# Inverting a delta rule's 16-row blocks: a DRAM scratch and substitution on GpSimd, or selecting products and substitution on VectorE

## The chip, the cores and the metric

The kernel runs on one core of one Trainium2 chip. The metric is the device time of one execution, in microseconds. A core has five engines with an instruction queue each, in order: TensorE (PE, with its weight loads PEld), VectorE (DVE), ScalarE (ACT), GpSimd (POOL) and SyncE (SP), which issues most of the DMAs. An instruction that waits holds up everything behind it on its engine.

## What is computed

Two layers on a sequence of 256 tokens of width 1024. Each layer has a half-step gated feed-forward (FFN1), a mixing sub-layer, and another feed-forward (FFN2), each with its modulation (shift, scale and gate from a product of a small vector with `w_ada`). The mixing sub-layer projects its normalised input once and gives the columns to three groups of heads:

```python
u_conv, u_moba, u_gdn = jnp.split(u, [IN_CONV, IN_CONV + IN_MOBA], axis=-1)
y_conv = conformer_conv(u_conv, ...)         # gated, causal depthwise convolution of 31 taps, LayerNorm, silu
y_moba = moba_attention(partial_rope(mq, pos), partial_rope(mk, pos), mv)        # 6 heads of 64
qkv = jax.nn.silu(causal_depthwise_conv(qkv, gdn_conv_w))                        # 4 taps
o = gated_delta_net(l2norm(gq), l2norm(gk), gv, g, beta)                         # 6 heads of 64
```

The gated delta net works in four chunks of 64 tokens. With `decay` from the cumulated g of a chunk, it needs for each head and chunk the inverse T of a unit lower triangular 64x64 matrix:

```python
L = jnp.where(strict, jnp.einsum('bhncd,bhnsd->bhncs', k_beta, k) * decay, 0.0)
T = lax.linalg.triangular_solve(eye + L, jnp.broadcast_to(eye, L.shape), left_side=True, lower=True)
u = T @ v_beta
```

## The kernel before

Weights stream from DRAM in 1 MB pieces (`raw`) through SP's queue; four such buffers are in use. ACT rounds each piece to a high half (`hi`) and DVE subtracts it for the low half (`lo`), and PE takes three products of the halves (H is the input's). Products of the input projection that feed the delta rule are whole (`pm<-Y,raw`, fp32). In the feed-forward parts that is nearly all the work. In the mixing sub-layer, PE's projections are the carrier and the rest is woven in between.

The order of all instructions is fixed when the program is built, by a list scheduler. The class `Clock` (l. 80 to 174) keeps a modelled time of each engine and DMA queue; `cost` (l. 117) prices an instruction. In `mixing` (l. 1010) twelve generators stand beside the projections (`sides`, l. 1656): `key_norms`, `query_norms`, `decays`, `pairs`, `gate_conv`, `values_beta`, `inverse`, `delta_rule`, `attention`, two of `taps` and `convolution`. Between two matmul groups, `tick` (l. 1660) lets each of them go on whose awaited tiles are ready by the modelled clock. So prices and waits in the generators set where an instruction stands on its engine; at run time each engine goes through its list.

The parts that the change touches:

- `decays` (l. 1197) makes the decay factors of all heads: three products of the triangle `kc` with g (`spread`, tiles `Lb` and `S6a`, DVE), matmuls with `gt`, `ones` and `identb`, and 18 exponentials on ACT into `PT`. It begins when the keys' norm is done (`until("g", "kh")`).
- `pairs` (l. 1257) has PE multiply keys by keys for each head (`pa<-S3a`); DVE multiplies the result by the decay into `LD` and `LX` (the tile `xin_LT`). Then it writes the 32x32 diagonal blocks of L, 12 of them in each of 4 groups of 32 partitions, to a DRAM scratch `scr_l`, by 4 DMAs from POOL's queue.
- `inverse` (l. 1367) reads each 16x16 diagonal block back, by 2 DMAs, into one lane: `Lb` has 96 lanes of 256 numbers. POOL masks the off-diagonal 16-blocks (`Um`), then does forward substitution in all lanes at once, 15 steps of a product `T<-W,Lb` and a subtraction `W<-W,T`. The inverses and their transposes go to `scr_w` by 4 DMAs and come back block-diagonal as `Wc` by 2. From there PE joins 16-blocks to 32 (`pa<-Wc,Lb`) and 32 to 64 by small products.
- `taps` (l. 1523) does the long convolution, 31 taps for each of two tiles. A tap is one operation on DVE (`cacc<-hc,colB,cacc`), or a scaled copy on ACT (`ctap`, two buffers) and an addition on POOL (`cacc<-cacc,ctap`); the modelled clocks choose. While the substitution is on POOL, `cfg["lo_pool"]` holds the taps to DVE.
- `scr_w` is zeroed once, after the first feed-forward.

Other names: `v`, `Q` and `S3a` are the delta rule's value, query and key channels in their short convolution; `H` x8 on DVE are the low halves of the mixing input; `E` are the attention's exponentials, `F` and `V` tiles of its last product; `adaacc` and `px` are the next modulation's product, `mod` its result; `g_g` is g in the delta rule.

## Time and profile before

| | |
|---|---|
| time, three runs | 1201.04, 1201.66, 1204.4 us; median 1201.66 |
| profiled execution | 1202.57 us, its span 1200.8 us |
| mean granted TensorE clock | 0.976 |
| busy: PE, DVE, ACT, POOL | 1130.7, 874.4, 612.6, 169.3 us |
| mixing sub-layer, layer 1 and 2 | about 233 to 464, and 815 to 1030 us |
| POOL from the first write of scr_l to the last read, layer 1 and 2 | 298.9 to 334.3, and 880.8 to 916.6 us |

All instructions are recorded through one helper, so each row of the profile has line L171, and groups are told apart by their tiles: `out<-in`. A row of a timeline has its start, its length, the engine, the operation, the count of like instructions in a row (x2), and in brackets the engine's idle time ahead of it with what ended that time. A matmul of whole 32-bit numbers shows as two records of the profile. A window has its length, the busy time of each engine with its count of instructions, the clock that TensorE was granted (1.00 is full), the DMA share and the rate.

### The profile page before, as it was taken

The numbers are of one execution on the slowest core, as the hardware profiler recorded it, in microseconds if no ns is written. First come the engines' busy times: TensorE is split into PE (matmuls) and PEld (weight loads), VectorE is DVE, ScalarE is ACT, GpSimd is POOL, SyncE is SP. The second block draws the span as 40 slices with busy tenths as digits, with TensorE's granted clock in tenths as the row PEclk, the third lists the DMA queues.
The fourth block names the chain that finished last, engine by engine and source line by source line (L and its number), as shares of the span: only waits on it lengthen the run. The fifth ranks groups of instructions, "written<-read, shape, count | busy, mean of one in ns | idle before, by whom it ended". The sixth has DMA issues, their size and how long they took to land.

```text
span 1200.8 us, 22053 instructions
## 1 busy us (share of the span) xinstructions
PE 1130.7 (94%) x9085; PEld 1052.0 (88%) x9085; DVE 874.4 (73%) x1314; ACT 612.6 (51%) x1049; POOL 169.3 (14%) x213
## 2 busy tenths in 40 slices
...
GB/s 320 246 186 319 309 299 309 256 113 192 95 137 91 176 176 285 322 243 326 291 218 170 324 313 266 278 300 74 186 140 73 141 108 140 287 257 211 195 139 36
DMA packets 167661, 256.52 MB, mean 214 GB/s; under 512 B 8272, under 2 KB 134056, under 8 KB 167560
## 3 DMA queue, kind: packets, MB, share of 16 engines
...
q0 software_dynamic: 1024, 2.16, 0.9%
...
q14 instruction: 30, 0.25, 0.1%
...
## 4 chain that ended last, share of the span: by engine, by line
PE 71%; DVE 12%; ACT 6%; POOL 6%; issue 3%; DMA 1%; SPq 0%; POOLq 0%; DVEq 0%; ACTq 0%
PE pm L171 45%; PE pa L171 25%; DVE lo L171 3%; DVE adaacc L171 3%; PE px L171 2%; ACT hi L171 1%; POOL W L171 1%; POOL cacc L171 1%; POOL T L171 1%; POOL Lb L171 1%; DVE mod L171 1%; ACT L171 1%; DVE tmp L171 1%; DVE Lb L171 1%; DVE Y L171 1%
## 5 line engine op out<-in xcount | busy, mean ns | idle before, releaser
L171 PE MATMUL pm<-H,hi 128*128 128x256 f32 x2816 | 507.7, 283 | 2.8 <-issue 1.6
L171 DVE TENSOR_TENSOR lo<-raw,hi 128x1024 fp32r<-128x1024 f32 (+1 forms) x300 | 362.1, 1226 | 131.8 <-ACT hi L171 131.3
L171 PEld LDWEIGHTS pm<-H,hi 128*128 128x128 f32 x2816 | 431.9, 189 | 5.9 <-issue 2.2
L171 ACT CAST hi<-raw 128x1024 fp32r<-128x1024 f32 (+1 forms) x306 | 311.3, 1040 | 195.3 <-PE pm L171 80.7
L171 PE MATMUL pm<-H,lo 128*128 128x256 f32 x1408 | 392.4, 280 | 1.2 <-DVE lo L171 1.2
L171 PEld LDWEIGHTS pm<-H,lo 128*128 128x128 f32 x1408 | 264.5, 189 | 1.7 <-DVE lo L171 1.6
L171 PE MATMUL pa<-Y,hi 128*128 128x256 f32 x1312 | 241.3, 286 | 4.5 <-DVE xT L171 4.5
L171 PEld LDWEIGHTS pa<-Y,hi 128*128 128x128 f32 x1312 | 204.1, 192 | 6.7 <-DVE xT L171 5.3
L171 PE MATMUL pa<-Y,lo 128*128 128x256 f32 x656 | 185.8, 283 | 0.0
L171 PEld LDWEIGHTS pa<-Y,lo 128*128 128x128 f32 x656 | 127.3, 194 | 0.0
L171 POOL TENSOR_TENSOR xin_LT<-xin_LT 128x256 f32<-128x256 f32 x35 | 27.1, 775 | 664.8 <-ACT xin_LT L171 662.4
L171 ACT CAST Y<-tmp 128x256 fp32r<-128x256 f32 x88 | 35.8, 406 | 131.5 <-DVE tmp L171 131.5
L171 DVE SCALAR_TENSOR_TENSOR adaacc<-raw,c_act,adaacc 128x1024 f32<-128x1024 f32 x70 | 95.5, 1365 | 1.6
L171 DVE SCALAR_TENSOR_TENSOR Lb<-raw,c_act,Lb 128x1024 f32<-128x1024 f32 x56 | 71.8, 1283 | 4.2 <-DMA raw<-in_w_ada_dram 3.0
L171 POOL TENSOR_TENSOR cacc<-cacc,ctap 128x256 f32<-128x256 f32 x54 | 52.3, 973 | 122.0 <-DVE cacc L171 112.8
L171 DVE TENSOR_TENSOR Y<-tmp,Y 128x256 fp32r<-128x256 f32 x88 | 37.4, 425 | 41.5 <-ACT Y L171 41.5
L171 PE MATMUL pm<-Y,raw 128*128 128x256 f32 x288 | 66.8, 384 | 0.0
L171 PEld LDWEIGHTS pm<-Y,raw 128*128 128x128 f32 x288 | 53.4, 190 | 8.9 <-issue 1.0
L171 PE MATMUL pa<-hi,Y 128*128 128x512 f32 x176 | 54.8, 393 | 0.0
L171 ACT ACTIVATE tmp<-pm 128x256 f32<-128x256 f32 x84 | 31.8, 378 | 43.9 <-PE pm L171 43.7
L171 DVE TENSOR_REDUCE mod<-px 128x4 f32<-128x512 f32 x34 | 23.4, 689 | 34.3 <-PE px L171 34.2
L171 DVE SCALAR_TENSOR_TENSOR cacc<-hc,colB,cacc 128x256 f32<-128x256 f32 x66 | 36.0, 562 | 10.3 <-POOL cacc L171 9.4
...
## 6 DMA issues: line engine op xcount, KB each, us to landing
...
```

The lines of the kernel that those rows point to most:

```text
L171: return getattr(real, op)(*args, **kw)
```

## The change

No DRAM scratch is left, and none of its 24 DMAs of the two layers or the 2 that zero it. A block gets into its lane by products on PE that select. DVE multiplies L's blocks by a mask (`blk16`: which 16 rows a partition belongs to), which puts each block's rows apart in a column of its own, `S6a`; 16 matmuls against `sel` then gather row i of all 96 blocks. Back, the inverse is spread by the masks `col8` (three products on DVE, one on POOL) and gathered by 16 matmuls against `col12`; two scaled copies on DVE (`half`) and a transpose by 32x32 blocks give `Wc`. The masks add 48 columns to the constants.

The 16-block is split into two 8-blocks, whose substitution takes 7 steps for both at once, with DVE in place of POOL; two products of 512 numbers a lane, each with a sum over the innermost axis, give the off-diagonal 8-block. The masks `Um` are now scaled copies on ACT. `decays` begins with the keys' convolution (`kconv`) and waits for the norm's table (`ktable`) ahead of its exponentials and for `kh` ahead of its last table load. `lo_pool` isn't toggled any more, and some prices in `cost` are others: ACT, POOL, and DVE's small operations.

```diff
...
+    k[:, o["sel"]:o["sel"] + 16] = i[:, None] % 16 == np.arange(16)[None, :]
+    k[:, o["blk16"]:o["blk16"] + 8] = i[:, None] // 16 == np.arange(8)[None, :]
+    k[:, o["half"]:o["half"] + 2] = i[:, None] % 32 // 16 == np.arange(2)[None, :]
+    k[:, o["col12"]:o["col12"] + 12] = i[:, None] // 8 == np.arange(12)[None, :]
+    k[:, o["col8"]:o["col8"] + 8] = i[:, None] % 8 == np.arange(8)[None, :]
...
             rows = 4 * max(m, n) if kind == F32 else max(2 * m, n) if kind == F32R else max(64, n)
             return 0.0065 + rows * 0.000435
         if engine == "act":
-            return 0.1 + n * 0.00082 if n > 400 else 0.1 + n * 0.0011
+            return 0.1 + n * 0.00092 if n > 400 else 0.12 + n * 0.0013
         if engine == "gp":
-            return max(0.17, 0.08 + n * 0.00222)
+            return max(0.17, 0.08 + n * 0.0035)
         if op == "reciprocal":
             return 0.07 + n * 0.0063
-        return 0.11 + n * 0.00113 if op == "scalar_tensor_tensor" else 0.13 + n * 0.00105
+        return 0.11 + n * 0.00113 if op == "scalar_tensor_tensor" else 0.13 + n * 0.00105 if n > 64 else 0.22
 
...
@@ -1003,8 +1010,6 @@
         return closing(acc, [key + ("d", f) for f in last], [hp(f) for f in last], gate, following)
 
 
-    scr_l = nc.dram_tensor("scr_l", [12, 4, 32, 32], F32, kind="Internal").ap()
-    scr_w = nc.dram_tensor("scr_w", [2, 12, 4, 32, 32], F32, kind="Internal").ap()
     late = {}
 
     def mixing(l, G, normed, nxt):
@@ -1179,6 +1184,7 @@
 
             def back():
                 act.preload_act_table_set("natural_log_exp_and_others")
+                ev["ktable"] = True
                 yield from ()
 
             yield from norms((kh[:, 0:2], kh[:, 2:3]), lambda: act.preload_act_table_set("silu_and_others"), back, 1.0)
@@ -1195,7 +1201,7 @@
             ev["qh"] = True
 
         def decays():
-            yield from until("g", "kh")
+            yield from until("g", "kconv")
             g, lnbeta = ev["g"], ev["lnbeta"]
             while any(job[1].tensor.name.startswith("Lb") for job in ada_wait):
                 extract()
@@ -1227,6 +1233,7 @@
                     mm(x, onesr, R[:, :, k, 1], k == 0, k == 1)
                 if b == 0:
                     spread(2)
+                yield from until("ktable")
                 yield (x,)
                 let_go(d)
                 let_go(x)
@@ -1236,6 +1243,7 @@
                     act.activation(PT[:, h, 128:256], x[:, s], AF.Exp, bias=cross[:, h:h + 1])
                     act.activation(PT[:, h, 256:384], d[:, s, 1], AF.Exp, bias=lnbeta[:, 1, NH + h:NH + h + 1])
                     ev["decay", h] = True
+            yield from until("kh")
             act.preload_act_table_set("silu_and_others")
             ev["silu2"] = True
 
@@ -1260,10 +1268,6 @@
                 yield from until(("decay", h))
                 yield (kh, PT[:, h])
                 yield from products(h, kh)
-            yield (LD,)
-            for q in range(4):
-                c = slice(32 * q, 32 * q + 32)
-                qd.dma_start(out=scr_l.rearrange("g b j i -> b j g i")[q], in_=LD.rearrange("p h t x -> p (h t) x")[c, :, c])
             ev["LT"] = True
             yield from until("qh")
             for h in range(NH):
@@ -1354,8 +1358,8 @@
                 dve.tensor_tensor(w[:, 0], og[:, b], h[:, 0], op=OP.subtract)
             ev["gdn_done"] = True
 
-        W = sb([96, 2, 16, 16], "W")
-        sp.dma_start(out=W[:, 0].rearrange("p c i -> p (c i)"), in_=t["konst"][0:96, K_OFF["winit"]:K_OFF["winit"] + 256])
+        W = sb([96, 272], "W")
+        sp.dma_start(out=W[:, 0:256], in_=t["konst"][0:96, K_OFF["winit"]:K_OFF["winit"] + 256])
         QUAD = [slice(32 * q, 32 * q + 32) for q in range(4)]
 
         def put(dst, src, scale=1.0):
@@ -1369,36 +1373,72 @@
 
 
             yield from until("LT")
-            cfg["lo_pool"] = False
             buf = sb([128, 1024], "Lb")
-            Lb = buf[0:96, 0:256].rearrange("p (j i) -> p j i", i=16)
-            Um, X = (buf[:, o:o + 384].rearrange("p (m i) -> p m i", i=32) for o in (256, 640))
...
+            Um, X = (buf[:, o:o + 384].rearrange("p (m i) -> p m i", i=32) for o in (384, 0))
+            LM = LD.rearrange("p h t x -> p (h t) x")
+            gp.memset(Um[:, :, 0:16], 0.0)
             yield (LD,)
-            LM = LD.rearrange("p h t x -> p (h t) x")
+
+            def pair_up(x):
+
+                return x.rearrange("p (s y) -> p s y", s=2)[:, :, 0:128].rearrange("p s (c i) -> p s c i", i=16)[:, :, 0:8, 0:8]
+
+
+            E = sb([128, 16, 12, 8], "S6a")
+            blocks = LM.rearrange("p m (b i) -> p i m b", i=16)
+            for c in range(4):
+                n = slice(4 * c, 4 * c + 4)
+                dve.tensor_tensor(E[:, n], blocks[:, n], K["blk16"].unsqueeze(1).unsqueeze(1).to_broadcast([128, 4, 12, 8]), op=OP.mult)
             for q in QUAD:
...
+                act.activation(Um[q, :, 16:32], LM[q, :, q.start + 16:q.stop], AF.Copy, scale=K["half"][q, 0:1])
+            yield (E[:, 0:8],)
+            yield from room()
+            p = pside([96, 16, 16], True)
+            for i in range(16):
+                mm(p[:, i], E[:, i].rearrange("p m b -> p (m b)"), K["sel"], True)
+            yield soon(p, "dve")
+            let_go(p)
+            U = buf[0:96, 0:272]
+            dve.tensor_scalar(U[:, 0:256], p.rearrange("p i j -> p (i j)"), -1.0, None, op0=OP.mult)
+            V = W[:, 0:256].rearrange("p (c i) -> p c i", i=16)
+            V2, U2 = pair_up(W), pair_up(U)
+            for j in range(7):
+                n, ni = j + 1, 7 - j
+                T = sb([96, 2, n, ni], "T", bufs=2)
+                dve.tensor_tensor(T, V2[:, :, 0:n, j:j + 1].to_broadcast([96, 2, n, ni]),
+                                  U2[:, :, n:8, j:j + 1].rearrange("p s i o -> p s o i").to_broadcast([96, 2, n, ni]), op=OP.mult)
+                dve.tensor_tensor(V2[:, :, 0:n, n:8], V2[:, :, 0:n, n:8], T, op=OP.add)
+            U = U[:, 0:256].rearrange("p (i j) -> p i j", j=16)
+            cube, half8 = [96, 8, 8, 8], sb([96, 8, 8], "T", bufs=2)
+            for n in range(2):
+                x = tmp([128, 2, S]).rearrange("p a s -> p (a s)")[0:96].rearrange("p (c i a) -> p c i a", c=8, i=8)
+                if n == 0:
+                    dve.tensor_tensor(x, V[:, 0:8, 0:8].unsqueeze(2).to_broadcast(cube), U[:, 8:16, 0:8].unsqueeze(1).to_broadcast(cube), op=OP.mult)
+                else:
+                    dve.tensor_tensor(x, half8.unsqueeze(2).to_broadcast(cube),
+                                      V[:, 8:16, 8:16].rearrange("p b i -> p i b").unsqueeze(1).to_broadcast(cube), op=OP.mult)
+                dve.tensor_reduce(V[:, 0:8, 8:16] if n else half8, x, axis=AX.X, op=OP.add)
+
             C = sb([128, 2, 12, 32], "Wc")
...
+            F = sb([96, 12, 8, 16], "S6a"), tmp([128, 2, S]).rearrange("p a s -> p (a s)")[0:96].rearrange("p (i b c) -> p i b c", i=4, b=8)
+            VT = V.rearrange("p c i -> p i c")
+            Fs = []
+            for c in range(4):
+                x = F[0][:, 4 * c:4 * c + 4] if c < 3 else F[1]
+                Fs.append(x)
+                (gp if c == 3 else dve).tensor_tensor(
+                    x, VT[:, 4 * c:4 * c + 4].unsqueeze(2).to_broadcast([96, 4, 8, 16]),
+                    K["col8"][0:96].unsqueeze(1).unsqueeze(3).to_broadcast([96, 4, 8, 16]), op=OP.mult)
+            yield (Fs[1],)
+            yield from room()
+            p = pside([128, 16, 12], True)
+            for i in range(16):
+                mm(p[:, i], Fs[i // 4][:, i % 4].rearrange("p b c -> p (b c)"), K["col12"][0:96], True)
+            yield soon(p, "dve")
+            let_go(p)
+            for n in range(2):
+                dve.tensor_scalar(C[:, 0, :, 16 * n:16 * n + 16], p.rearrange("p i m -> p m i"), K["half"][:, n:n + 1], None, op0=OP.mult)
+            dve.transpose(C[:, 1].rearrange("p m i -> p (m i)"), C[:, 0].rearrange("p m i -> p (m i)"))
             yield from until("kh")
             wide = sb([128, 1536], "S6a")
             TA, X64 = (wide[:, o:o + 768].rearrange("p (m i) -> p m i", i=64) for o in (0, 768))
...
```

Three places in the order. First, DVE in layer 1 about the convolution of the queries (`Q`) and keys (`S3a`), where the products of `kc` and `g_r` (`Lb`, `S6a`) are those of `decays`. Before:

```order
L171 TENSOR_SCALAR adaacc<-raw,c_act 128x1024
L171 SCALAR_TENSOR_TENSOR adaacc<-raw,c_act,adaacc 128x1024
...
L171 SCALAR_TENSOR_TENSOR Q_2761<-pm_2816,colB,Q_2761 128x253 x2
L171 TENSOR_TENSOR lo<-raw,hi 128x1024
L171 TENSOR_TENSOR S3a<-S3a,tmp_2835 128x512
L171 TENSOR_TENSOR lo<-raw,hi 128x1024
L171 TENSOR_TENSOR S3a<-S3a,tmp_2841 128x256
L171 TENSOR_TENSOR Lb<-kc,g_r 128x1024
L171 TENSOR_TENSOR S6a<-kc,g_r 128x1024
L171 TENSOR_TENSOR g_c<-pa_2901,g_x 128x6
L171 TENSOR_TENSOR lo<-raw,hi 128x1024
L171 TENSOR_TENSOR Lb<-kc,g_r 128x1024
```

After:

```order
L178 SCALAR_TENSOR_TENSOR Q_2757<-tmp_2760,colB,Q_2757 128x253
L178 TENSOR_TENSOR Lb<-kc,g_r 128x1024
L178 TENSOR_TENSOR S6a<-kc,g_r 128x1024
L178 TENSOR_TENSOR g_c<-pa_2819,g_x 128x6
L178 TENSOR_SCALAR adaacc<-raw,c_act 128x1024
L178 SCALAR_TENSOR_TENSOR adaacc<-raw,c_act,adaacc 128x1024
...
L178 SCALAR_TENSOR_TENSOR Q_2757<-pm_2812,colB,Q_2757 128x253 x2
L178 TENSOR_TENSOR S3a<-S3a,tmp_2833 128x512
L178 TENSOR_TENSOR Lb<-kc,g_r 128x1024
L178 TENSOR_TENSOR lo<-raw,hi 128x1024
L178 TENSOR_TENSOR S3a<-S3a,tmp_2840 128x256
```

The first two products and the sum `g_c` have moved ahead of the modulation's step `adaacc` and of the taps of `Q` on `pm`, and the third ahead of the weights' `lo`.

Second, DVE from the last of the pairs' products (`xin_LT`) to the low halves `H` and the taps of `v`. Before:

```order
L171 TENSOR_SCALAR cacc<-hc,colB,colA 128x256 x2
L171 TENSOR_TENSOR xin_LT<-pa_3041,PT 128x256
L171 TENSOR_TENSOR xin_LT<-pa_3041,PT 128x128
L171 TENSOR_TENSOR H_2815<-Y,H_2814 128x256 x8
L171 SCALAR_TENSOR_TENSOR v<-pm_2998,colB,v 128x255 x2
L171 SCALAR_TENSOR_TENSOR v<-pm_2998,colB,v 128x254 x2
L171 SCALAR_TENSOR_TENSOR v<-pm_2998,colB,v 128x253 x2
```

After:

```order
L178 TENSOR_TENSOR xin_LT<-pa_3006,PT 128x256
L178 TENSOR_TENSOR xin_LT<-pa_3006,PT 128x128
L178 TENSOR_TENSOR S6a<-xin_LT,kc 128x384 x4
L178 SCALAR_TENSOR_TENSOR adaacc<-raw,c_act,adaacc 128x1024 x2
L178 TENSOR_TENSOR hc<-hc,V 128x2x256
L178 TENSOR_SCALAR Lb<-pa_3038 96x256
L178 TENSOR_TENSOR T<-W,Lb 96x14
L178 TENSOR_TENSOR W<-W,T 96x2x7
...
L178 TENSOR_TENSOR W<-W,T 96x2x7
L178 TENSOR_TENSOR tmp_3084<-W,Lb 96x512
L178 TENSOR_REDUCE T<-tmp_3084 96x64
```

```order
L178 TENSOR_TENSOR tmp_3087<-T,W 96x512
L178 TENSOR_REDUCE W<-tmp_3087 96x8x8
L178 TENSOR_TENSOR S6a<-W,kc 96x512 x3
L178 TENSOR_TENSOR H_2811<-Y,H_2810 128x256 x8
L178 SCALAR_TENSOR_TENSOR v<-pm_3031,colB,v 128x255 x2
L178 SCALAR_TENSOR_TENSOR v<-pm_3031,colB,v 128x254 x2
L178 SCALAR_TENSOR_TENSOR v<-pm_3031,colB,v 128x253 x2
L178 TENSOR_SCALAR cacc<-hc,colB,colA 128x256 x2
```

Between the last pair and `H` there now stand the four masked copies, the two `adaacc` that stood among the pairs, the 14 steps, the two products with their sums and the three selecting products; the gate `hc` and the first taps of `cacc` have moved behind the pairs, `cacc` behind taps of `v`.

Third, PE in the same place, from the last pair (`pa<-S3a`) to the first products of the attention's query projection (`pm<-H,hi`). Before:

```order
L171 MATMUL pa_3041<-S3a 128x256
L171 MATMUL pa_3041<-S3a 128x128
L171 MATMUL pm_2998<-Y,raw 128x256 x9
L171 MATMUL pm_3099<-Y,raw 128x256 x8
L171 MATMUL pm_3117<-H_2814,hi 128x256
L171 MATMUL pm_3117<-H_2815,hi 128x256
L171 MATMUL pm_3117<-H_2814,lo 128x256
```

After:

```order
L178 MATMUL pa_3006<-S3a 128x256
L178 MATMUL pa_3006<-S3a 128x128
L178 MATMUL pm_2948<-Y,raw 128x256 x3
L178 MATMUL pm_3031<-Y,raw 128x256 x2
L178 MATMUL pa_3038<-kc,S6a 96x16 x16
L178 MATMUL pm_3031<-Y,raw 128x256 x14
L178 MATMUL pm_3134<-Y,raw 128x256 x8
L178 MATMUL pm_3155<-H_2810,hi 128x256
L178 MATMUL pm_3155<-H_2811,hi 128x256
L178 MATMUL pm_3155<-H_2810,lo 128x256
L178 MATMUL pa_3159<-kc,S6a 128x12 x12
L178 MATMUL pa_3159<-kc,tmp_3092 128x12 x4
```

The pair stands ten projection matmuls earlier, with the 16 selecting matmuls of 96 rows among them, and the 16 of 128 rows stand behind the query projection's first group. Also on PE, the product of `g_g` with `gt` (6 columns) is now right behind the first matmul `pm<-Y,raw` of its stretch, where before it stood behind 26 of them. On POOL each layer's taps are 16 where they were 27, and its queue has no DMA.

36 lines of the change are left out of this document (6 added, 30 removed).

## Prediction

> **What bounds the kernel now.** I read the page's busy shares and chain first, then the windows of whole stretches, then the timeline of PE with the idle time ahead of each row.
>
> ```profile
> PE 1130.7 (94%) x9085; PEld 1052.0 (88%) x9085; DVE 874.4 (73%) x1314; ACT 612.6 (51%) x1049; POOL 169.3 (14%) x213
> PE 71%; DVE 12%; ACT 6%; POOL 6%; issue 3%; DMA 1%; SPq 0%; POOLq 0%; DVEq 0%; ACTq 0%
> ...
> 464.00:620.00 156.00, 154.12 (x1307) 153.51 (x1306) 120.80 (x145) 69.40 (x96) 0.00 (x0) 1.00 0.83 289
> 300.88:405.22 104.34, 91.53 (x981) 77.24 (x979) 74.83 (x137) 61.17 (x129) 47.58 (x68) 0.97 0.35 111
> 882.70:991.64 108.94, 96.63 (x992) 82.28 (x991) 75.44 (x139) 61.76 (x130) 47.53 (x68) 0.91 0.35 108
> ```
>
> The columns of a window are its length, then busy time of PE, PEld, DVE, ACT and POOL, then the granted clock. PE is the bound, and in the feed-forward stretch (464 to 620) it is full at clock 1.00, so nothing is to be had there. The second and third windows run, in layer 1 and layer 2, from the first matmul of the attention's query projection to the first of the next modulation (px). PE's work there at full clock is busy time times clock: 91.53 x 0.97 = 88.8 us, and 96.63 x 0.91 = 87.9 us. The losses are therefore 104.34 - 88.8 = 15.5 and 108.94 - 87.9 = 21.0 us. What ends the idle part of them is in PE's timeline:
>
> ```profile
> 307.56 0.76 PE L171 MATMUL pa<-kc,v 128*128 128x128 f32 x3 [2.01 <-ACT v L171]
> 345.16 1.09 PE L171 MATMUL pa<-kc,E 128*128 128x128 f32 x3 [4.73 <-ACT E L171]
> 356.85 1.25 PE L171 MATMUL pa<-F,V 128*64 128x256 f32 x8 [2.07 <-ACT V L171]
> 409.15 0.66 PE L171 MATMUL px<-kc,adaacc 128*128 128x128 f32 x4 [3.33 <-DVE mod L171]
> ...
> 927.48 1.08 PE L171 MATMUL pa<-kc,E 128*128 128x128 f32 x3 [6.37 <-ACT E L171]
> ```
>
> The largest wait, once in each layer, is for the softmax's E on ACT. Its origin is POOL, which does the 16-block substitution between two trips through DRAM:
>
> ```profile
> 298.93 2.48 POOL L171 DMA_DIRECT2D scr_l<-xin_LT  x4
> 305.68 1.46 POOL L171 DMA_DIRECT2D Lb<-scr_l  x2 [4.27 <-PE pa L171]
> 311.67 0.28 POOL L171 TENSOR_TENSOR T<-W,Lb 96x15 f32<-96x15 f32 x1
> 326.22 0.61 POOL L171 COPY W<-W 96x256 f32<-96x256 f32 x1
> 332.26 2.07 POOL L171 DMA_DIRECT2D Wc<-scr_w  x2 [2.56 <-DMA scr_w<-W]
> 335.46 0.51 ACT L171 ACTIVATE ctap<-hc,colB 128x256 f32<-128x256 f32 x1 [7.84 <-POOL cacc L171]
> 339.15 0.96 DVE L171 TENSOR_TENSOR lo<-raw,hi 128x768 fp32r<-128x768 f32 x1 [7.27 <-ACT hi L171]
> ```
>
> From 298.93 to 334.33 (332.26 + 2.07) POOL does nothing but the inverse. An ACT instruction of the long convolution (ctap) stands in ACT's order and waits until POOL takes up its taps again; behind it stand E, on which PE waits at 345.16, and the cast hi, on which DVE waits at 339.15. So the price of the DRAM route isn't its own latency but ACT held for 7.84 us.
>
> **What the change removes.** The two trips, the 30 substitution steps, the four masks and the copy leave POOL, and with them the wait of ctap. The most that can come back is the two losses, 15.5 + 21.0 = 36.5 us, and the wait of px at 409.15, 3.33 us, which stands at the end of the gated norm's chain on DVE in layer 1 only: **39.9 us**. (Layer 1's later DVE chain from 411.44 to 420.65, seven products adaacc, stays as it is in both orders.)
>
> **What it adds on PE.** 32 matmuls of 96 or 128 rows by 16 or 12 columns a layer.
>
> ```profile
> 977.28 1.52 PE L171 MATMUL pm<-vb,xin_LT 128*128 128x64 f32 x12 [0.15 <-DVE vb L171]
> 338.17 1.02 PE L171 MATMUL pa<-Wc,Lb 32*32 32x32 f32 x96
> 259.08 10.96 PE L171 MATMUL pm<-Y,raw 128*128 128x256 f32 x50
> 261.07 0.17 DVE L171 TENSOR_TENSOR g_g<-g_x,g_ea 128x12 f32<-128x12 f32 x1
> ```
>
> The nearest full-height rows take 1.52 / 12 = 0.13 us each; the packed small ones 1.02 / 96 = 0.01. Full height is nearer: 32 x 0.13 = 4.2 a layer, **8.4 us** in all (bounds 0.6 and 8.4). The product of g_g with gt now is second in the stretch that began at 259.08, right behind one matmul of 0.43 us (10.96 / 25), so PE is there at 259.5 and g_g is done at 261.24: a new wait of 1.8 us a layer, **3.6 us** (bounds 0, if the later start is given back, and 3.6).
>
> **What it adds on DVE.** The prices:
>
> ```profile
> 259.17 1.27 DVE L171 SCALAR_TENSOR_TENSOR g_q<-g_q,g_e 128x24 f32<-128x24 f32 x6
> 322.97 0.56 DVE L171 TENSOR_TENSOR PT<-pa,PT 128x384 f32<-128x384 f32 x1 [0.26 <-PE pa L171]
> 330.32 0.69 DVE L171 TENSOR_TENSOR Y<-Y,tmp 128x512 f32<-128x512 f32 x1
> 343.76 0.43 DVE L171 STREAM_SHUFFLE tmp<-Y 128x256 f32<-128x256 f32 x1
> 358.13 0.48 DVE L171 SCALAR_TENSOR_TENSOR cacc<-hc,colB,cacc 128x256 f32<-128x256 f32 x1
> L171 DVE TENSOR_REDUCE mod<-px 128x4 f32<-128x512 f32 x34 | 23.4, 689 | 34.3 <-PE px L171 34.2
> L171 POOL TENSOR_TENSOR cacc<-cacc,ctap 128x256 f32<-128x256 f32 x54 | 52.3, 973 | 122.0 <-DVE cacc L171 112.8
> ```
>
> Four block products of 384 are 4 x 0.56 = 2.2; the copy out of PSUM about 0.4 (half of the 512 row and a little); 14 dependent small steps at 1.27 / 6 = 0.21 are 3.0; two products of 512 and two reductions 4 x 0.69 = 2.8; three products of 512 are 2.1; two scaled copies and a transpose, priced by the 384 row and the shuffle, 1.6. That is 12.1 us, and in each layer 11 taps of the long convolution go from POOL (27 before, 16 now) to DVE, 11 x 0.48 = 5.3. So DVE has 74.83 + 17.4 = 92.2 us to do in a stretch in which PE has 88.8 + 4.2 = 93.0. Some comes off again: taps on DVE take a mean 562 ns in the page against 0.48 beside a quiet POOL, 33 x 0.08 = 2.7 us. Both engines would have to be full for the whole loss to come back. I don't expect that.
>
> [...]
>
> **Where PE will wait now.** I walked layer 1 in the changed order with these durations. The pairs' products come earlier, since the decays no longer stand behind the norm: 27 matmuls of 0.43 us and the 16 selecting ones now lie between the last pair and the first query matmul, so the last pair leaves PE about 291, the block products end near 294, the substitution 300, the reductions 303, the last selecting products 305. Behind them on DVE are the eight low halves of h and the nine short-convolution taps of v:
>
> ```profile
> L171 DVE TENSOR_TENSOR Y<-tmp,Y 128x256 fp32r<-128x256 f32 x88 | 37.4, 425 | 41.5 <-ACT Y L171 41.5
> ...
> 295.07 0.73 DVE L171 TENSOR_SCALAR cacc<-hc,colB,colA 128x256 f32<-128x256 f32 x2
> ...
> 296.25 4.36 DVE L171 TENSOR_TENSOR H<-Y,H 128x256 fp32r<-128x256 f32 x8
> 300.53 2.42 DVE L171 SCALAR_TENSOR_TENSOR v<-pm,colB,v 128x255 f32<-128x255 f32 x6
> 303.78 1.51 DVE L171 SCALAR_TENSOR_TENSOR v<-pm,colB,v 128x255 f32<-128x255 f32 x3
> 304.96 0.59 PE L171 MATMUL pa<-tmp,kc 128*128 128x256 f32 x2
> 305.00:310.00 5.00, 2.99 (x9) 1.45 (x9) 4.66 (x8) 4.56 (x6) 4.16 (x5) 0.78 0.43 132
> ```
>
> H begins near 305 where it began at 296.25. The first query matmul, at 300.88 before, comes at 305.3 (1.8 us for g_g, 2.1 for the first 16 selecting matmuls, 0.5 until the last block product), so H is just in time. H takes 8 x 0.425 = 3.4 us, to 308.4; nine taps of v at 2.42 / 6 = 0.40 and the two first taps of the long convolution, 0.73, end at 312.8; PE came 2.3 us behind the last tap before (307.56 less 303.78 + 1.51), which makes 315.1. PE is there at 312.1: its start, 4.1 for the 36 query matmuls (300.88 to 304.96), 2.1 for the other selecting ones and 0.6. That is a wait of 3.0 us. Walked on in the same way, the query's taps make it wait 0.5, the products PT (each holds a PSUM buffer until DVE has read it, and its reading stands between the taps) 3.0 and 1.5, the rotary of the second pair of heads 2.2: 10.2 us a layer, **20.4 us**, half of what was removed. The bounds: 2 us a layer, v's wait alone as in before; and 14, with two more waits like the 2.07 at 356.85 near the stretch's end.
>
> Clock: at 305 to 310 a wait of 2.01 us came with 0.78 on 2.99 us of matmuls, 0.66 us lost. One such a layer is **1.3 us** (bounds 0, and 17, twice layer 2's 96.63 - 87.9 = 8.7). [...]
>
> **The sum.** -39.9 + 8.4 + 3.6 + 20.4 + 1.3 = -6.2 us on the profiled span of 1200.8, so 1194.6. The profiled execution took 1202.57 and the runs have a median of 1201.66, which is 0.9 above the span: **1195.5 us**.
>
> **The rivals.** *All hidden.* DVE's new work slips between PE's products, v's wait stays as it was (2 us a layer), g_g costs nothing: -39.9 + 8.4 + 4 + 1.3 = -26, 1175 us. For it: DVE idles 7.27 us at 339 and 29.5 in the stretch. Against it: 92.2 less 2.7 of DVE beside 93.0 of PE, in orders that depend on each other step by step.
>
> *DVE becomes the bound.* In-order DVE puts 14 dependent steps, four products of 512 and 44 taps ahead of what PE asks for; every product PT, H and v comes later than I walked, and the clock falls with each wait. At 14 us of waits and 4 of clock a layer: -39.9 + 8.4 + 3.6 + 36 = +8, 1210 us. It decides from the point where waits and clock exceed 13.9 us a layer ((39.9 - 12.0) / 2). For it: DVE was already the fuller of the two in 305 to 310 (4.66 against 2.99). Against it: POOL's taps, slow as they are (973 ns), now run beside it unblocked.
>
> *The wait only moves.* ACT is freed from POOL, so E's waits of 4.73 and 6.37 us go, and px's 3.33. The other losses stay: v and V are ACT's work behind DVE's, which the change leaves as it was. With the 12.0 us on PE paid, that is -14.4 + 12.0 + 2 (the clock of as many short waits as before, and E's rest) = 0, 1201 us. Speaks for it that v made PE wait 2.01 us although POOL had nothing to do with it; against it that V at 356.85 stood behind the delayed taps.
>
> **How the numbers follow.** A measurement here tells about 0.3%, 3.6 us, from no change. Chances: the forecast 0.45 (1187 to 1202), all hidden 0.20, DVE the bound 0.22, the wait only moves 0.13. Faster: 0.20 and seven tenths of the forecast, 0.52. Slower: 0.22 and a little of the last, 0.25. The same: 0.23. The range, 1177 to 1210, leaves out most of the best case's lower half and the worst of DVE.
>
> **What would show it.** In the changed profile: POOL without DMAs and ctap without a wait over 3 us; the E matmuls 96x16 near 293 to 295; the first query matmul near 305; a wait of PE near g_g of 1.8 us; pa<-kc,v waiting some 3 us for ACT's v, the products Q,S3a for DVE's PT; px of layer 1 near 406.6, since 15.5 us go and 16.9 come, but without its 3.33; layer 2's stretch 4 us shorter, 21.0 going. If PE's waits between the query's start and px sum to over 14 us a layer, or the clock there is under 0.93, the forecast is wrong towards slower; under 5 us, towards faster.

## The result

The changed kernel takes **1216.03 us** (median; 1211.03 to 1218.31), the kernel before beside it 1201.35 (1200.86 to 1204.4). The ratio is 1.0108, with a 95% interval of 1.0074 to 1.0142: about 1% slower, where 1195.5 was predicted. The profiled execution took 1218.31 us with a span of 1216.2, against 1202.57 and 1200.8 before.

The page of the changed kernel, its busy shares and the shares of the chain:

```profile
PE 1152.9 (95%) x9213; PEld 1076.1 (88%) x9213; DVE 892.8 (73%) x1380; ACT 611.1 (50%) x1047; POOL 94.4 (8%) x98
PE 77%; DVE 15%; ACT 4%; issue 2%; DMA 1%; SPq 0%; POOL 0%; POOLq 0%; DVEq 0%; ACTq 0%
```

POOL has left the chain (6% before). PE's idle time, span less busy, fell from 1200.8 - 1130.7 = 70.1 us to 1216.2 - 1152.9 = 63.3. Yet the span grew by 15.4: PE is busy for 22 us longer. Windows of its work show why. They hold layer 1 from the first query matmul to the wait ahead of px, two pieces of it, and the same stretch of layer 2:

```profile
303.70:414.67 110.97, 106.02 (x1018) 93.02 (x1016) 76.91 (x158) 60.77 (x129) 14.71 (x18) 0.83 0.25 86
306.88:320.90 14.02, 14.02 (x68) 14.02 (x69) 9.54 (x24) 3.92 (x4) 2.64 (x4) 0.52 0.13 45
334.46:357.00 22.54, 22.54 (x200) 18.30 (x201) 14.80 (x34) 7.82 (x22) 4.76 (x6) 0.50 0.10 25
896.90:1010.20 113.30, 108.54 (x1064) 95.22 (x1062) 82.33 (x163) 65.55 (x135) 14.78 (x18) 0.86 0.28 92
```

The two stretches have a granted clock of 0.83 and 0.86, where before they had 0.97 and 0.91. In two pieces of layer 1, 14 and 22.5 us long, PE has no gap at all and runs at half clock. PE's timeline shows what stands ahead of them:

```profile
259.80 0.39 PE L178 MATMUL pa<-g_g,gt 128*128 128x6 f32 x2 [1.61 <-DVE g_g L178]
...
291.64 2.81 PE L178 MATMUL pa<-kc,S6a 128*96 128x16 f32 x32
...
306.88 0.58 PE L178 MATMUL pm<-H,hi 128*128 128x256 f32 x1 [2.71 <-DVE H L178]
307.26 0.42 PE L178 MATMUL pm<-H,lo 128*128 128x256 f32 x1
307.48 5.13 PE L178 MATMUL pa<-kc,S6a 96*128 96x12 f32 x24
312.45 1.86 PE L178 MATMUL pa<-kc,tmp 96*128 96x12 f32 x8
...
319.42 0.63 PE L178 MATMUL pm<-H,hi 128*128 128x256 f32 x2
319.85 0.41 PE L178 MATMUL pm<-H,lo 128*128 128x256 f32 x1
...
320.54 0.40 PE L178 MATMUL pm<-H,hi 128*128 128x256 f32 x2
320.77 0.28 PE L178 MATMUL pm<-H,lo 128*128 128x256 f32 x1
...
334.46 1.64 PE L178 MATMUL pa<-Q,S3a 64*128 64x256 f32 x4 [1.95 <-DVE PT L178]
...
418.49 0.66 PE L178 MATMUL px<-kc,adaacc 128*128 128x128 f32 x4 [3.82 <-DVE adaacc L178]
```

A wait of 2.71 us for H is followed by the 16 selecting matmuls of 12 columns (two records each) and by half clock until 320, where the projection's pair of products goes from 0.63 and 0.41 back to 0.40 and 0.28. A wait of 1.95 us for PT is followed by matmuls of 64 and 32 rows and by half clock until 357. Layer 2 is alike: a wait of 2.73 us for H and one of 1.74 us ahead of the joins `pa<-Wc,Lb`, each with half clock behind it. The waits for E and v, 4.73 and 2.01 us before, are gone; that of px is not. DVE in layer 1 has the substitution, then the selecting products beside POOL's, then H:

```profile
299.32 0.18 DVE L178 TENSOR_TENSOR W<-W,T 96x14 f32<-96x14 f32 x1
299.53 0.69 DVE L178 TENSOR_TENSOR tmp<-W,Lb 96x512 f32<-96x512 f32 x1
...
302.63 3.86 DVE L178 TENSOR_TENSOR S6a<-W,kc 96x512 f32<-96x512 f32 x3
306.42 2.75 DVE L178 TENSOR_TENSOR H<-Y,H 128x256 fp32r<-128x256 f32 x8
...
302.85 1.92 POOL L178 TENSOR_TENSOR tmp<-W,kc 96x512 f32<-96x512 f32 x1 [24.76 <-DVE W L178]
```

To split the span I sum windows of 2 us over all of it, in the prediction's terms: idle, clock loss (busy time times one less the clock), and the rest, PE's work at full clock.

| us | before | changed | difference |
|---|---|---|---|
| idle | 70.1 | 63.3 | -6.8 |
| clock loss | 22.3 | 43.8 | +21.5 |
| work at full clock | 1108.4 | 1109.1 | +0.7 |

The last row is rough: of three kernels with the same matmuls (before, e15 and e18 below) it gives 1108.4, 1102.5 and 1100.4. So it can't show whether PE's work grew by some 10 us or not at all.

### The profile page after: what moved, and what is told of

It is laid out like the page before. It is cut to its first block, busy times and chain, and to the rows that moved or that the text cites. A ratio compares the mean times of both kernels' runs of the same rounds, so it can differ in the third digit from the quotient of the medians.

```text
span 1216.2 us, 22216 instructions
## 1 busy us (share of the span) xinstructions
PE 1152.9 (95%) x9213; PEld 1076.1 (88%) x9213; DVE 892.8 (73%) x1380; ACT 611.1 (50%) x1047; POOL 94.4 (8%) x98
## 4 chain that ended last, share of the span: by engine, by line
PE 77%; DVE 15%; ACT 4%; issue 2%; DMA 1%; SPq 0%; POOL 0%; POOLq 0%; DVEq 0%; ACTq 0%
PE pm L178 47%; PE pa L178 29%; DVE lo L178 3%; DVE adaacc L178 3%; PE px L178 2%; ACT hi L178 1%; DVE tmp L178 1%; DVE S6a L178 1%; DVE mod L178 1%; DMA raw<-in_w_in_dram 1%; DVE H L178 1%; DVE PT L178 1%; DVE Lb L178 1%; DMA xin_LT<-in_x_dram 1%; DVE cacc L178 1%
## 5 line engine op out<-in xcount | busy, mean ns | idle before, releaser
L178 PE MATMUL pm<-H,hi 128*128 128x256 f32 x2816 | 515.2, 285 | 6.7 <-DVE H L178 6.7
L178 PEld LDWEIGHTS pm<-H,hi 128*128 128x128 f32 x2816 | 437.6, 192 | 10.0 <-DVE H L178 7.5
L178 PEld LDWEIGHTS pm<-H,lo 128*128 128x128 f32 x1408 | 268.2, 191 | 1.9 <-DVE lo L178 1.9
L178 PE MATMUL pa<-Y,hi 128*128 128x256 f32 x1312 | 237.6, 284 | 3.9 <-DVE xT L178 3.2
L178 DVE SCALAR_TENSOR_TENSOR cacc<-hc,colB,cacc 128x256 f32<-128x256 f32 x88 | 44.3, 535 | 3.8 <-POOL cacc L178 3.1
L178 DVE TENSOR_TENSOR tmp<-tmp,pm 128x256 f32<-128x256 f32 x80 | 33.1, 414 | 10.4 <-ACT tmp L178 10.4
```

Source lines behind the costliest of these rows:

```text
L178: return getattr(real, op)(*args, **kw)
```

## Experiments

Two questions: is it the clock that costs the time, and what brings it down; and which part of the change does it, for it has three: the new inverse, the early decays, and the prices in the planner's cost table. Medians of the kernels before beside these runs were 1200.6 to 1201.5 us, so their times can be set side by side.

| run | what it is | median us | ratio to before, 95% |
|---|---|---|---|
| e1 | changed, dense matmuls in H's wait | 1215.33 | 1.0114 (1.0088 to 1.0140) |
| e5 | changed, dense matmuls in PT's wait | 1205.18 | 1.0020 (0.9995 to 1.0045) |
| e13 | changed, both | 1200.34 | 0.9990 (0.9974 to 1.0007) |
| e2 | changed, H ahead of the substitution | 1192.41 | 0.9922 (0.9897 to 0.9948) |
| e4 | changed, back products later | 1208.13 | 1.0064 (1.0042 to 1.0087) |
| e8 | e2, back products spread | 1218.77 | 1.0141 (1.0091 to 1.0191) |
| e10 | e2, wide selecting products | 1194.40 | 0.9952 (0.9936 to 0.9969) |
| e11 | e10, dense matmuls in px's waits | 1192.89 | 0.9938 (0.9923 to 0.9953) |
| e12 | changed, wide selecting products | 1214.86 | 1.0113 (1.0093 to 1.0133) |
| e6 | before, 16 small matmuls more | 1201.62 | 0.9998 (0.9984 to 1.0013) |
| e7 | before, 7 dense matmuls more | 1203.95 | 1.0019 (1.0004 to 1.0033) |
| e9 | before, 48 small matmuls more | 1214.03 | one run |
| e3 | changed, decays late again | 1209.47 | 1.0072 (1.0046 to 1.0099) |
| e14 | changed, old prices | 1216.53 | 1.0104 (1.0061 to 1.0147) |
| e15 | before, new prices | **1172.72** | 0.9769 (0.9753 to 0.9784) |
| e16 | before, new prices, early decays | 1187.58 | 0.9893 (0.9868 to 0.9917) |
| e17 | e15, 16 small matmuls more | 1179.10 | 0.9802 (0.9780 to 0.9824) |
| e18 | before, POOL's new price alone | 1192.01 | 0.9912 (0.9890 to 0.9935) |

### Filling the waits: e1, e5, e13

Added matmuls, here and in e6, e7, e9, e11 and e17, give results that nothing reads. In e1, seven of them (`FILL`) stand ahead of the first query product of each layer:

```diff
+                for _ in range(FILL if b == 0 else 0):
+                    nc.tensor.matmul(o[:, 0], ident, whole_h[:, 0], start=True, stop=True, skip_group_check=True)
```

> The changed kernel with seven matmuls of 128x256 more in each layer, ahead of the attention's first query product, into the PSUM tile that this product then overwrites: 7 x 0.43 = 3.0 us of PE work in place of the wait for H of 2.71 us. Nothing else moves. Clock theory (the loss is half clock after short PE waits behind DVE): the stretch at half clock from 306.88 to 320.5 in layer 1 is gone, the 16 matmuls of 12 columns take about 3.3 us and not 6.7, some 7 us saved a layer; 1202 us, and less (1185 to 1195) if the later wait for PT was a child of it. Work theory (PE and DVE have simply more to do and the clock follows what PE does): no gain, 1214 to 1220.

No gain. H's wait is gone, but the clock halves all the same, in PE's timeline right behind the selecting products and with no gap ahead of them:

```profile
304.19 3.19 PE L1770 MATMUL pm<-Y,kc 128*128 128x256 f32 x14
307.02 0.60 PE L179 MATMUL pm<-H,hi 128*128 128x256 f32 x2
307.46 0.28 PE L179 MATMUL pm<-H,lo 128*128 128x256 f32 x1
307.57 2.74 PE L179 MATMUL pa<-kc,S6a 96*128 96x12 f32 x24
310.17 1.04 PE L179 MATMUL pa<-kc,tmp 96*128 96x12 f32 x8
311.06 0.61 PE L179 MATMUL pm<-H,hi 128*128 128x256 f32 x2
```

At full clock the 16 take 311.06 - 307.57 = 3.5 us, where the changed kernel has 6.7 at half. Half clock is only 3.4 us here (6.8 in layer 2), but PT's place is nearly as bad as before (a wait of 2.17 us, then 20.5 us at half). In e5 five dense matmuls stand ahead of the product that waits for PT, and five at the matching place of layer 2:

```diff
+            if rhs is qh and h == 3 and l == 0:
+                dense(5)
...
+            if l == 1:
+                dense(5)
```

> The changed kernel with five matmuls of 128x256 (2.2 us) into an idle PSUM tile in each layer, where PE waited 1.95 us in layer 1 (ahead of the fourth product Q,S3a) and 1.74 us in layer 2 (ahead of the second Wc,Lb). Nothing else moves on any engine. Idle theory (half clock follows an idle PE of about 2 us): the 22 us at half clock behind this place in each layer are gone, 11 us a layer, 1192 to 1198 us. Activity theory (half clock follows some 3 us in which the array had little to do, idle or busy with small matmuls): behind the filled place stand 24 matmuls of 32x32 and the scores with 64 rows, so the clock still falls, a few us later; 1206 us or more.

10.8 us less than the changed kernel, so PT's place seems to be most of the loss. In the profiled execution, the fastest of the ten, the half clock behind H is shorter too (3.4 us in place of 13.7 in layer 1), so how much is PT's place alone isn't shown. e13 has both fills.

> Changed kernel with both fills at once: the seven dense matmuls ahead of the first query product in each layer and the five at the place of the wait for PT, none of which is read. Clock theory: the two places are separate losses and each is a matter of the clock; together the fills should bring the clock loss of 43.8 us down to before's 22 or below, less some 5 us of added work that no wait hides: 1200 to 1205 us. Rival (the fill at H only moves the fall, as the single fill there showed): no better than the fill at PT alone, 1203 to 1207 us with the clock still down some 3.4 to 6.6 us behind the selecting matmuls. If it comes out above 1208, the fill at H costs its own work.

1200.34, as the clock theory had it. Together the fills gain 15.7 us, all of the 14.7 by which the changed kernel is slower than the kernel before, although they add 24 matmuls. Windows of layer 1's two places and of both stretches from the query's start to px:

```profile
305.00:310.00 5.00, 5.00 (x33) 4.57 (x31) 5.00 (x10) 0.87 (x2) 1.19 (x1) 1.00 0.88 301
340.00:345.00 5.00, 5.00 (x52) 4.68 (x51) 4.27 (x10) 4.92 (x14) 2.66 (x3) 1.00 0.12 23
308.11:406.06 97.95, 91.96 (x1029) 80.46 (x1027) 77.80 (x159) 59.91 (x127) 14.69 (x17) 1.00 0.27 92
890.61:990.64 100.03, 99.74 (x1070) 88.72 (x1069) 78.35 (x160) 64.22 (x132) 14.14 (x17) 0.97 0.28 94
```

The clock is 1.00 and 0.97 where it was 0.83 and 0.86. Work is added and time goes: the loss was the clock's.

### The order on DVE: e2, e4, e8

e2 makes the inverse wait until H is issued, so that H and six taps of v precede the substitution on DVE:

```diff
+            yield from until("lows")
             yield soon(p, "dve")
...
+            ev.update(lows=True) if i else None
             o = bank()
```

> The changed kernel, but the copy out of PSUM ahead of the substitution waits until the eight low halves H have been issued; so on DVE H stands ahead of the 14 steps and the selecting products and not behind them. Clock theory: the wait for H and its half clock are gone, 1190 to 1202 us. Work theory: DVE does the same work, the wait moves to v or Wc, 1212 or more.

1192.41, 0.8% faster than the kernel before. DVE's order, PE's back products and the two stretches:

```profile
304.00 2.82 DVE L178 TENSOR_TENSOR H<-Y,H 128x256 fp32r<-128x256 f32 x5
306.74 2.41 DVE L178 SCALAR_TENSOR_TENSOR v<-pm,colB,v 128x255 f32<-128x255 f32 x6
309.08 0.40 DVE L178 TENSOR_SCALAR Lb<-pa 96x256 f32<-96x256 f32 x1
...
318.76 1.06 PE L178 MATMUL pa<-kc,S6a 96*128 96x12 f32 x8 [0.86 <-DVE S6a L178]
...
305.60:405.72 100.12, 93.31 (x1018) 80.07 (x1016) 81.07 (x159) 63.04 (x133) 26.23 (x25) 0.96 0.29 99
884.40:985.25 100.85, 98.24 (x1060) 86.34 (x1059) 82.02 (x160) 67.13 (x138) 24.20 (x25) 0.97 0.30 101
```

The waits for H and PT are gone; the clock loss of the whole span is 16.3 us in place of 43.8. e4 keeps DVE's order and lets the back products go behind some 24 query matmuls.

```diff
+            yield lambda: "query" in ev and clock.t["pe"] >= ev["query"] + 5.0
             yield from room()
```

> The changed kernel, but the second 16 selecting matmuls stand behind 24 matmuls of the query projection (128x128 by 256) and not behind 3. The wait for H stays. If half clock lasts until PE has had some 3.5 us of full-size matmuls in a row: it ends about 311 in place of 320.5, the selecting matmuls take 3.3 us and not 6.7, some 4 to 5 us a layer, 1206 to 1208. If its length after a wait doesn't depend on what PE does: about 14 us again, 1214 to 1218.

In layer 1 H's wait stays at 2.71 us, but the clock falls only 6 us later, when the small matmuls come (in layer 2 within 1 us of the wait's end). The half clock behind PT's place and its match in layer 2 shrinks from 23.9 and 20.5 us to 6.8 and 13.7. 7.9 us less than the changed kernel. e8 takes e2 and lets one back product at a time go between projection matmuls:

```diff
                 mm(p[:, i], Fs[i // 4][:, i % 4].rearrange("p b c -> p (b c)"), K["col12"][0:96], True)
+                yield
```

> The kernel with the low halves first, and the 16 selecting matmuls of the way back issued one or two at a time between the query projection's matmuls in place of 16 in a row. Activity theory: the half clock behind them (about 321 to 328 in layer 1, 899 to 905 in layer 2) is gone or shorter, 1186 to 1190 us. Idle theory: only the short waits between them (1.4 us a layer) can be won, and Wc comes later: 1190 to 1194.

A miss, 26 us worse than e2. The inverse ends later, and PE then waits for its products, with half clock at 379 to 399 and 955 to 966. Spreading the small matmuls didn't help here.

### What brings the clock down: e6, e7, e9, e10, e11, e12

These put matmuls into the kernel before, in e6 16 of 96 rows by 12 columns a layer ahead of the query projection, in e7 seven dense ones, in e9 48 small ones (e6's edit):

```diff
+                for _ in range(16 if b == 0 else 0):
+                    nc.tensor.matmul(o[:, 0, 0:12], kc[0:96, 0:128], kc[0:96, 128:140], start=True, stop=True, skip_group_check=True)
```

> The kernel before with 16 matmuls of 96 rows by 12 columns more in each layer, ahead of the attention's first query product, where PE is full at clock 1.00; they depend on nothing late, so PE doesn't idle. Activity theory: the clock falls to half behind them for 3 to 7 us; 3.3 us for the matmuls and 2 to 4 for the clock in each layer, 1211 to 1215. Idle theory: clock 1.00, 3.3 us a layer, 1207.

> The counterpart: the kernel before with 7 matmuls of 128x128 by 256 columns at the same place, 3.0 us of PE work of full size. Both theories: clock stays at 1.00 there, 3.0 us a layer, 1206 to 1207. If the time itself or the place brings the clock down, it falls here as well.

> The kernel before with 48 matmuls of 96 rows by 12 columns at the place where sixteen brought the clock down in neither layer: some 10.5 us in which PE never idles and the array gets few columns. Activity theory (the clock is set window by window of about 3.4 us, by what the array got, and a busy PE with small matmuls counts as idle): at least one whole window lies inside, so the clock falls to 0.50 in both layers before the 48 are through, or right behind them. Idle theory: clock 1.00 throughout, since PE has no idle time there.

16 small matmuls left the clock at 1.00 here and cost nothing in the end. In the window in which PE was 2.99 of 5.00 us busy before, waiting for v at a clock of 0.78, it now has no gap:

```profile
305.00:310.00 5.00, 5.00 (x39) 4.37 (x38) 4.89 (x6) 4.59 (x7) 4.62 (x6) 1.00 0.12 28
```

Seven dense ones cost 2.4 us. With 48 small ones, e9's timeline and windows settle a point:

```profile
301.12 17.30 PE L1729 MATMUL pm<-kc 96*128 96x12 f32 x96
318.27 0.77 PE L171 MATMUL pm<-H,hi 128*128 128x256 f32 x2
...
321.90 0.28 PE L171 MATMUL pm<-H,lo 128*128 128x256 f32 x1
...
305.00:310.00 5.00, 5.00 (x25) 5.00 (x25) 4.86 (x7) 3.41 (x3) 4.76 (x6) 0.50 0.35 106
310.00:315.00 5.00, 5.00 (x25) 5.00 (x25) 0.78 (x1) 0.00 (x0) 3.99 (x14) 0.50 0.00 0
```

PE is busy without a gap, 5.00 of 5.00 us, and the clock is 0.50. It comes back at 321.7, some 3.4 us after dense products begin. In e9 the clock needs no idle time that the profile shows (it models the ends of matmuls) to fall: 17.3 us of small matmuls are enough. In e1, 16 of them behind dense work did it; in e6 they didn't.

e10 asks whether it is their few columns, and repeats the columns of the moving operand to 96 and 120, so that each matmul streams more; what a later one overwrites isn't read. e12 does it in the changed kernel, e11 adds nine dense matmuls (`fill`, the last two lines) ahead of two px in layer 1:

```diff
-                mm(p[:, i], E[:, i].rearrange("p m b -> p (m b)"), K["sel"], True)
+                mm(wp[:, 16 * i:16 * i + 96], E[:, i].rearrange("p m b -> p (m b)"), K["sel"].unsqueeze(1).to_broadcast([128, 6, 16]), True)
...
+        for _ in range(cfg.get("fill", 0) if h == 0 else 0):
+            nc.tensor.matmul(p.rearrange("p j n -> p (j n)")[:, 0:256], ident, xT[:, 0], start=True, stop=True, skip_group_check=True)
```

> The kernel with the low halves first (1192.4 us), and the selecting matmuls with their moving columns repeated, 120 in place of 12 and 96 in place of 16; the surplus columns land where the next matmul writes. The order is unchanged on every engine; a matmul's own time should stay near 0.2 us, since the weight load sets it. Activity theory: the half clock behind them (321 to 328 in layer 1, 899 to 905 in layer 2, some 3 us each) is gone, 1186 to 1190 us. Idle theory: unchanged or 1 us slower, 1192 to 1194.

> The same, and in layer 1 nine matmuls of 128x256 (3.9 us) into the PSUM tile of px ahead of each of the two transposes that waited 3.99 and 5.21 us for DVE's adaacc. Activity theory: the half clock behind these two waits (3.5 and some 5 us of matmuls at 0.50) goes, 2 to 4 us less than the kernel without them. Idle theory: the same, since here PE does idle.

> The changed kernel itself with the wide selecting matmuls, its order unchanged. H is late as before (wait 2.7 us). Activity theory: the half clock behind that wait lasts one or two windows (3.4 to 6.8 us) in place of 13.6, since the 16 matmuls behind it count as work now; the second half clock, behind PT, stays; 4 to 5 us less a layer, 1206 to 1209 us. If the wait alone sets it: 1214 to 1217.

No gain in time over e2 in e10, though in its profiled execution, the fastest of the four, the half clock behind the back products is 0 and 3.4 us in the two layers where e2 has 6.8 in each. e12 shortens the half clock behind H from 13.7 to 10.2 us in layer 1 and from 10.2 to 6.8 in layer 2, leaves that of PT's place at 44.4 us in both layers together, and gains 1 us, a miss. In e11 the waits of px are 0.78 and 2.15 us where e2 has 3.99 and 5.21, and the time is 1.5 us below e10's, within the scatter.

By their times, then, these runs don't say what measure of PE's work the clock follows. The kept traces say more. In each of the 20, the stretches at half clock begin on one grid of 3.41 us, whose place differs from trace to trace, and last one to eight of its steps (unless the trace ends first). In the kernel before they begin at 307.76, 345.31 and 925.58 us, among others, 11 and 170 steps apart, and last 3.41, 3.41 and 10.24 us; in the changed kernel at 306.64, 333.95, 900.56 and 924.46, lasting 13.65, 23.89, 10.24 and 20.48. Two windows of e1's grid, with the 16 small matmuls and behind them, and the one behind most of them in e6:

```profile
307.85:311.26 3.41, 3.41 (x32) 3.41 (x32) 3.41 (x11) 0.00 (x0) 0.00 (x0) 1.00 0.27 89
311.26:314.67 3.41, 3.41 (x17) 3.41 (x17) 3.31 (x10) 1.17 (x2) 1.81 (x3) 0.50 0.00 0
...
305.10:308.51 3.41, 3.41 (x29) 3.29 (x28) 3.30 (x4) 3.03 (x4) 3.18 (x4) 1.00 0.16 36
```

For each window I count the columns that PE's matmuls stream in it, each matmul's times its share of 128 rows, a whole product as four of rounded halves (0.43 us against 0.12); the unit is a rounded product of 128 rows by 256 columns:

| window, from (us) | idle, us | count | clock behind it |
|---|---|---|---|
| before, wait for v (304.35) | 2.01 | 10.6 | 0.50 |
| changed, wait for H (303.23) | 2.48 | 7.9 | 0.50 |
| changed, wait for PT (330.54) | 1.44 | 10.4 | 0.50 |
| e4, wait for H, cut in two by the grid (304.19, 307.60) | 1.64, 1.07 | 15.7, 18.2 | 1.00, 1.00 |
| e1, 16 small (307.85) | 0 | 2.6 | 0.50 |
| e6, 16 small, cut in two (298.28, 301.69) | 0, 0 | 18.4, 12.9 | 1.00, 1.00 |
| e17, 16 small, layer 2 (872.93) | 0 | 10.2 | 0.50 |
| e2, back products (318.40) | 0.65 | 1.6 | 0.50 |
| e10, the same, 120 columns each (318.33) | 0.67 | 14.5 | 1.00 |

A count of 12 parts these rows. Over all 20 traces it is under 12 in 184 of the 190 windows behind which the clock falls and in 192 of the 201 behind which it stays at half, and over 12 in 169 of the 170 behind which it comes back and in all but 3 of the 6351 behind which it stays full. This is an estimate, worked out from the matmuls and clocks of these traces after the runs; no run was made to test it, and some of the 19 exceptions are far from the line (up to 17.5). By this estimate columns do count, and a wait costs clock or not by where the grid cuts it.

### The parts of the change: e3, e14 to e18

e3 gives the decays their old start, `yield from until("g", "kh")`; the rest is the changed kernel.

> The changed kernel with one part undone: decays begin behind the keys' norm as before. The substitution then falls behind H on DVE by itself, and g_g no longer holds PE for 1.6 us. Clock theory: the early decays are what put the substitution ahead of H; 1195 to 1205 us. Work theory: the early decays were a gain of their own, so without them 1218 or more.

6.6 us less, between the two theories' ranges. g_g and H make no wait, since the planner now finds H ready ahead of the substitution; the clock still falls behind short waits later. e14 has the changed kernel with the three old prices, e15 the kernel before with the three new ones (here e15's edit):

```diff
-            return 0.1 + n * 0.00082 if n > 400 else 0.1 + n * 0.0011
+            return 0.1 + n * 0.00092 if n > 400 else 0.12 + n * 0.0013
-            return max(0.17, 0.08 + n * 0.00222)
+            return max(0.17, 0.08 + n * 0.0035)
-        return 0.11 + n * 0.00113 if op == "scalar_tensor_tensor" else 0.13 + n * 0.00105
+        return 0.11 + n * 0.00113 if op == "scalar_tensor_tensor" else 0.13 + n * 0.00105 if n > 64 else 0.22
```

> Changed kernel with the three prices of the modelled clock as they were; the substitution still stands ahead of H on DVE. Order theory (the loss comes from where H and PT stand, not from the prices): H waits as before the edit, the time stays at 1210 to 1218 us. Rival (the new prices made the planner place taps so that DVE is late): 1200 to 1205 us.

> Kernel before with the three new prices alone: the taps move from POOL to DVE, everything else as it was. Order theory: POOL's inverse and the wait of ctap stay, no new PE wait behind DVE before the inverse; 1199 to 1205 us. Rival (the moved taps crowd DVE): over 1207 us with new waits of PE for v or PT.

e14's time is as expected, its way there isn't: H doesn't wait, and no wait of PE in this stretch is over 1.2 us. Some 3 us behind one of 0.66 us the clock falls, and PE runs 27 us at half:

```profile
332.46 0.92 PE L178 MATMUL pa<-Q,S3a 64*128 64x256 f32 x4 [0.66 <-DVE PT L178]
...
340.00:345.00 5.00, 5.00 (x26) 3.44 (x24) 4.96 (x13) 1.17 (x3) 0.00 (x0) 0.50 0.41 108
```

e15 is the surprise: **1172.72 us, 2.3% faster than before**, with POOL's substitution and its way through DRAM untouched. Neither theory had this. Its groups of taps, ACT's timeline, PE's, and the two stretches:

```profile
L171 POOL TENSOR_TENSOR cacc<-cacc,ctap 128x256 f32<-128x256 f32 x24 | 23.8, 993 | 154.4 <-DVE H L171 108.5 <-ACT ctap L171 29.2 <-DVE sm L171 9.0
...
328.58 0.37 ACT L171 ACTIVATE E<-pa,mx 128x128 f32<-128x128 f32 x1
...
336.38 0.49 PE L171 MATMUL pa<-kc,E 128*128 128x128 f32 x3
...
341.20 1.50 PE L171 MATMUL pa<-Wc,Lb 32*32 32x32 f32 x96 [3.99 <-DMA Wc<-scr_w]
...
298.83:391.40 92.57, 87.68 (x953) 75.15 (x951) 74.95 (x140) 54.03 (x113) 35.83 (x57) 0.93 0.37 122
867.43:964.39 96.96, 93.64 (x1009) 82.23 (x1008) 79.79 (x150) 57.76 (x121) 35.95 (x57) 0.95 0.40 129
```

POOL has 12 taps a layer where it had 27. No `ctap` stands in ACT's order ahead of E while POOL substitutes: E begins at 328.58 (337.50 before), and PE comes to it at 336.38 without a wait, where it had waited 4.73 us. The stretches are 11.8 and 12.0 us shorter than before. The whole span has 51.7 us of idle time and 16.0 of clock loss, against 70.1 and 22.3.

e18 changes POOL's price alone, e16 adds the early decays to e15, e17 adds e6's 16 small matmuls to e15.

> Kernel before with one price changed alone: a tap's addition on POOL at 0.98 us in the modelled clock in place of 0.65 (the profile of before has 0.973). It takes 9 taps a layer off POOL and 3 scaled copies a layer off ACT's order. If that wrong price is what put ctap in front of E, most of the gain of all three prices is here: 1172 to 1182 us, without a wait of ctap over 3 us. Rival (the prices of ACT and of the small operations on DVE are needed too): 1190 us or more, with ctap still held.

> Kernel before with the new prices and the earlier decays, its inverse through DRAM as it was. If the early decays do harm only because they let the substitution stand ahead of H on DVE, they are harmless with the substitution on POOL, and let the block's way through DRAM begin earlier: the wait of 3.99 us for Wc in layer 1 goes and the time is 1163 to 1172 us. Rival (the early decays themselves cost: PE's wait for g_g, 1.6 us a layer, and a clock that falls behind it): 1174 to 1182 us.

> Kernel before with the new prices and, beside the query projection of each layer, 16 matmuls of 96 rows by 12 columns that nothing reads. In the kernel before their 7 us were hidden by later waits; here those waits are gone. Theory (the selecting products' work on PE has no cover left once ACT is free): plus 5 to 9 us, 1178 to 1182 us, as much as each half of the selecting products costs in the changed kernel. Rival (still hidden by the wait of 3.99 us for Wc and the waits for E): 1171 to 1175 us.

e18 gains 9.3 us, a third. In layer 1 no `ctap` waits for over 1.2 us, but the first E come in two lots, at 324 and 344, short waits follow, and the clock is at half at 364 to 381 and 940 to 968. Neither theory's whole picture holds: the price of POOL frees ACT, the other two are needed for the rest.

e16 is 14.9 us slower than e15, more than the rival had. The wait for Wc is gone as hoped, but PE waits for g_g and for v, and DVE's rows say why:

```profile
259.40 0.39 PE L171 MATMUL pa<-g_g,gt 128*128 128x6 f32 x2 [1.62 <-DVE g_g L171]
...
309.07 0.90 PE L171 MATMUL pa<-kc,v 128*128 128x128 f32 x3 [3.50 <-ACT v L171]
...
294.92 2.57 DVE L171 SCALAR_TENSOR_TENSOR cacc<-hc,colB,cacc 128x256 f32<-128x256 f32 x5
297.40 2.77 DVE L171 TENSOR_TENSOR H<-Y,H 128x256 fp32r<-128x256 f32 x8
```

With the pairs done early, taps of the long convolution slip in ahead of H and among the taps of v; in e15 H is done at 296.3. So the early decays cost time without the new inverse too. e17 costs 6.4 us more than e15, as its theory had it: once ACT is free, half of the selecting products' work on PE has no cover.

## Why the prediction was wrong, step by step

**What bounds the kernel, and ACT's part: right in the main.** That the DRAM route costs by holding ACT at `ctap`, more than by its own latency, is what e15 bears out: the route stays, ACT is freed, 28.6 us go, and one wait of 3.99 us for `Wc` from DRAM is left. Not all of that is ACT's hold: e18, where no `ctap` of this stretch waits over 1.2 us, gains 9.3. What the prediction didn't see is that the new prices in the same diff do this alone. It priced the 11 taps that they move to DVE (5.3 us of DVE's work) and counted the freed ACT as a gain of the new inverse. One sign was wrong as well: in the changed kernel a `ctap` still waits 7.83 us for POOL, at 312.78, where no E stands behind it in time.

**The idle time: right in sum, by luck.** Of the 39.9 us removed, 12.8 and 12.3 were idle in the two stretches (their length less busy) and 3.3 px's wait, 28.4 in all; 3.6 and 20.4 were to come back: -4.4. Measured over the span: -6.8. But in the two stretches only 4.95 and 4.76 us are idle, 9.7 and not 20.4; what came out too low there was made up by longer waits of px and of others outside them. Single waits, with the forecast in brackets: g_g's was 1.61 (1.8). H, "just in time", made PE wait 2.71 and 2.73: three selecting products took 3.86 us (2.1 predicted) beside POOL's, whose 1.92 us overlap them. v's wait (3.0) didn't come, PT's was 1.95 (3.0). px waited 3.82, now behind DVE's adaacc, so its 3.33 were not gained; a later px of layer 1 waited 5.26 (3.80 before), and layer 2 has a new one of 2.46.

**DVE's steps: right.** The 14 small steps took 0.17 to 0.21 us each (0.21), the last ended at 299.5 (300), the reductions at 302.7 (303), and PE reached the first query matmul at 303.70 (305.3).

**The selecting products: undersized.** 2.66 us for the first 16 of a layer (291.64 to 294.30) and, at full clock, 3.5 for the others, 6.2 us a layer or 12.3 in all, against 8.4. At half clock the second 16 took 6.7. The row that priced them, 1.52 us for x12, holds two records for each matmul: six matmuls of 0.25 us and not twelve of 0.13. Read so, it gives 8.1 us a layer, as much too high as 4.2 was too low.

**The clock: this step failed.** The prediction took 2.7 + 8.7 = 11.4 us of the old clock loss as gained and gave 1.3 back, one wait like that of 2.01 us in each layer: -10.1. Measured over the span: +21.5, which is 31.6 us off. In the two stretches alone the clock now costs 106.02 x 0.17 + 108.54 x 0.14 = 33 us, where 1.3 was forecast and 17 was the bound. Work and idle together came out 10 us below their part of the sum, so that the span is at +15.4 and not at -6.2; half clock counted as a factor of 2 (it is 1.8, see below) and the rough work row are part of that.

Two things were wrong in the step. The price of one wait was read too low: behind the wait for v the clock is at half from 307.76 to 311.18, all of it busy, which is 1.7 us lost. The window from 305 to 310 ends too early, and its mean of 0.78 is taken over its idle part as well. And the row had a short wait in the midst of dense projection matmuls, and the clock was back after 3.41 us. Here a wait, or none, stands ahead of a run of small matmuls, and PE stays at half clock for 10 to 24 us. e13 shows that these two places are worth the whole slowdown.

Of the signs that the prediction had named for being wrong, a clock under 0.93 in these stretches is there (0.83 and 0.86). The other pointed the wrong way: PE's waits in them, without px's, are under 5 us a layer, which was to mean faster.

**The rivals.** *DVE becomes the bound* came nearest, 1210: it has H and PT late on DVE and the clock falling, but it gave waits 14 us a layer and the clock 4. What decided was the clock, not the waits. *All hidden* (1175) is, as it happens, near the time of e15, by another part of the change. *The wait only moves* (1201) kept the waits for v and V, and both are gone.

**Where the time went, by parts.** At the new prices: with the old inverse 1172.7, with early decays as well 1187.6; with the new inverse 1209.5, with both 1216.0. So the early decays cost 14.9 us or 6.6, and the new inverse 36.8 or 28.4. At the old prices the two together cost 15.2 (1201.3 to 1216.5). The gain of the prices, 28.6 us, is not there with the new inverse (1216.5 to 1216.0): PE has no wait for E over 0.6 us with the old prices either. Of the new inverse's cost some 12 us is PE's work by the rows above. Much of the rest is the clock, 43.8 us of loss by the split above against 16.0 in e15; the fills and e2 recover 16 and 24 us of it. The best kernel found is e15: it beats the kernel before by 2.3% and the changed one by 43 us.
